# A transformer block's attention on one core: scores and transposed probabilities move into shared PSUM banks

## The chip, the cores and the metric

The kernel runs on one core of a Trainium2 chip. The metric is the device time of one execution in microseconds; three timed runs of the kernel before gave 797.0, 797.51 and 798.45, median 797.51. A core has five engines with an instruction queue each: TensorE (PE, matmuls; PEld is its loading of weights), VectorE (DVE), ScalarE (ACT), GpSimd (POOL) and SyncE (SP, which here only issues DMA transfers). They run side by side and wait for each other by semaphores. Matmuls write to PSUM, which has eight banks of 512 fp32 numbers for each of the 128 partitions.

## The reference, cut to what matters

One layer on 512 tokens of 2048 numbers: a norm, sliding-window attention with a gate, a projection back, then a second stage that adds a gated embedding, and a last norm. The attention has 32 query heads in 4 groups of 8, each group with one head of keys and values, 64 numbers a head:

```python
q, k, v, gate = jnp.split(h @ w_in, [...], axis=-1)
scores = jnp.einsum('bnqhgd,bnjhd->bnhgqj', q, kb) * (SWA_HEAD_DIM ** -0.5) + bias
scores = jnp.where(mask, scores, jnp.finfo(jnp.float32).min)      # a window of 128 keys
m = jnp.maximum(scores.max(axis=-1, keepdims=True), sink)
e = jnp.exp(scores - m)
probs = e / (e.sum(axis=-1, keepdims=True) + jnp.exp(sink - m))
out = jnp.einsum('bnhgqj,bnjhd->bnqhgd', probs, vb).reshape(bsz, seq, SWA_WIDTH)
y = (out * jax.nn.silu(gate)) @ w_out
```

## The kernel before

**Precision.** Every fp32 operand is split into a high and a low part, and a product is three matmuls (`mm3`, L126 to L128). The split of a weight piece is one ScalarE cast (`whi`, L109) and one VectorE subtraction (`wlo`, L110).

**Stages.** A first stage projects keys, values and two query blocks (until about 70 us). Then come 30 more projection blocks of queries (`qps`) and gates (`gps`), each 16 times `mm3`: 40 of these `mm3` by themselves, and the other 432 but 8 as filling between the steps of attention, so that TensorE has work while the softmax runs on other engines. Behind attention (from about 450 us) stand the output projection, the embedding's stage and the last norm.

**Attention** has 64 blocks of work (4 key heads x 16 units of 32 query tokens x 8 heads). The loop at L909 makes 67 steps; step `i` issues, in this order:

- the value matmuls of an output block (`weigh`, L586, even steps): two passes, with the high and the low part of the transposed probabilities `r`;
- the transposes of block `i-2` (`turn`, L546), two matmuls on TensorE that write `pt`; ScalarE copies it as the high part of `r` (L557), VectorE subtracts for the low part (L558);
- the scores of block `i` (`scores`, L478), two matmuls into `s`, one bank each;
- VectorE's softmax on `s`: add the bias (L508), subtract and find the minimum (L511, one for each half), merge (L516); later ScalarE's exponentials (L522), VectorE's reciprocal (L524), ScalarE's scaling to `pr` (L533 to L537, in the step after);
- 6 `mm3` of the projections (7 from step 30 on), and between them, at places counted by `n`, a weight split, the second part of the output (`own`, L589), its evaluation (L598 on ScalarE, L600 on VectorE), and the **pieces**: what a finished projection block still needs on VectorE and ScalarE. A query block has three pieces: scale (`qps`, L325, VectorE), high part (`q`, L336, ScalarE), low part (L334, VectorE). A gate has three too (L630, L631, L624), and later a fourth. Pieces wait in two lists, `chores` and `idle`, and `some()` issues the first of a list. Before, a step issues one at n = 0, one at n = 2 if more than one waits, and one at n = 4.

The order of the work on all five engines is written out by this loop, and each engine runs its own instructions strictly in that order. The pool library puts in the semaphores.

**Banks.** Pool `psum` has two banks each for the tags `o`, `p` and `t` (outputs, projections, transposes); one more pool of two banks holds the scores: one set of two banks, used by every step.

**Sums of weights.** Some weights are added on the way (`sum_weights`, L688): SP copies 512 KB from HBM to HBM (L693), and GpSimd's queue adds a second block to it (L695). Eight of these copies are issued before attention (SUMS_EARLY = 16), the others in its steps. SP's queue holds the loads of weights (`wraw`, L102) as well.

Of the kernel before, what the change touches and what calls it, by code (L numbers as in the profile page):

```python
# [55 lines left out]
def trunk_kernel(ctx: ExitStack, tc: tile.TileContext, a: dict):  # L56
# [8 lines left out]
    psum = pool("psum", bufs=2, space=PSUM)  # L65

    banks_s = ExitStack()
    others = {"s": banks_s.enter_context(tc.tile_pool(name="psum_s", bufs=2, space=PSUM))}

    pn = const.tile([P, KC], F32, name="pn")  # L70

# [338 lines left out]

    pre.close()
    banks_s.close()
    spsum = mid.enter_context(tc.tile_pool(name="psum_w", bufs=1, space=PSUM))
    apool = mid.enter_context(tc.tile_pool(name="attn", bufs=1, reuse_waits="tile"))


# [1 line left out]

    U, T, PT, gates, biases = {}, {}, {}, {}, {}

    DV = apool.tile([P, NB - 1, 2, KVH * 2 * HD], F32R, name="DV")
    apool.tile([P, 8], F32, name="pad2")
# [36 lines left out]
    def scores(i):  # L461

        d, g = divmod(i, UNITS)
        if g == UNITS // 2 and d + 1 < KVH:
            load_bias(d + 1)
        of_keys = K[d].rearrange("p j l k -> p (j l k)")  # L470

        s_ps = spsum.tile([P, 2, S], F32, tag="w", name=f"s{i}")
        number = [min(2 * g + u + 1, GROUP + 1) * QB for u in range(2)]
        for u in range(2):
            first, n = max(2 * g + u - GROUP, 0), number[u]
            part, at = divmod(2 * g + u, S // QB // len(Q[d]))
            st = Q[d][part][:, at].rearrange("p h q -> p (h q)")
            nc.tensor.matmul(s_ps[:, u, : 2 * n], st, of_keys[:, first * 2 * QB : (first * QB + n) * 2], start=True, stop=True)  # L478
        W = KEYS + 2
        t = apool.tile([P, 2, W], F32, tag="t", name=f"t{i}", bufs=2)  # L480
        at = t[:, 0, 0:1]

        def two(of, stride, n):
            return bass.AP(tensor=at.tensor, offset=at.offset + of, ap=[at.ap[0], [stride, 2], [1, n]])

        def by_block(out, u, n):
            of = s_ps[:, u, : 2 * n].rearrange("p (j l k) -> p l j k", l=2, k=QB)
            return out.rearrange("p (j k) -> p j k", k=QB), of[:, 0], of[:, 1]

        late = QB if g >= P // TQ else 0  # L490
        seen = [t[:, 0, 0 : P + 1], t[:, 1, 1 + late : P + 2 + late] if late else t[:, 1, 0 : P + 1]]
        pr = [t[:, u, 1 + late * u : 1 + late * u + P] for u in range(2)]
        nc.gpsimd.tensor_copy(two(0, W + W - 1 if late else W, 1), sinkb[:, d : d + 1].unsqueeze(1).to_broadcast([P, 2, 1]))  # L493
        for u, n in enumerate(number):
            if n < P:
                nc.gpsimd.memset(t[:, u, 1 + n : 1 + P], -MASKED)
        yield
        bias = biases[d][:, ::-1]
        sm = apool.tile([P, 24], F32, tag="sm", name=f"sm{i}", bufs=4)
        if not late:  # L500
            for u, n in enumerate(number):
                blocks_of, high, low = by_block(t[:, u, 1 : 1 + n], u, n)
                nc.vector.tensor_add(blocks_of, high, bias[:, KEYS - n :].rearrange("p (j k) -> p j k", k=QB))
        else:
            x = t[:, :, 1 : 1 + KEYS].rearrange("p u (j k) -> p u j k", k=QB)
            of = s_ps[:, :, : 2 * KEYS].rearrange("p u (j l k) -> p u l j k", l=2, k=QB)
            spread = bias.rearrange("p (j k) -> p j k", k=QB).unsqueeze(1).to_broadcast([P, 2, KEYS // QB, QB])
            nc.vector.tensor_add(x, of[:, :, 0], spread)  # L508
        for u, n in enumerate(number):
            blocks_of, high, low = by_block(t[:, u, 1 : 1 + n], u, n)  # L510
            nc.vector.tensor_tensor_reduce(  # L511
                out=blocks_of, in0=low, in1=blocks_of, scale=-1.0, scalar=sinkb[:, d : d + 1], op0=ALU.add, op1=ALU.min,
                accum_out=sm[:, u : u + 1],
            )
        if late:
            nc.vector.tensor_tensor(  # L516
                out=two(1, W + P, QB), in0=t[:, :, 1 : 1 + QB], in1=t[:, :, 1 + P : 1 + KEYS], op=ALU.min
            )
        yield
        for u in range(2):  # L520
            su = seen[u]
            nc.scalar.activation(su, su, AF.Exp, scale=-1.0, bias=sm[:, u : u + 1], accum_out=sm[:, 2 + u : 3 + u])  # L522
        yield
        nc.vector.reciprocal(sm[:, 4:6], sm[:, 2:4])  # L524
        yield

        T[i] = apool.tile([P, 2, P], F32, tag="pr", name=f"pr{i}", bufs=2)
        for u in range(2):
            out, src, w = T[i][:, u], pr[u], sm[:, 4 + u : 5 + u]
            ahead = 2 * (g + u) % GROUP * QB if late else 0  # L530
            if ahead == P // 2:
                out = out.rearrange("p (h k) -> p h k", h=2)[:, ::-1]
                nc.scalar.mul(out, src.rearrange("p (h k) -> p h k", h=2), w)  # L533
            else:
                nc.scalar.mul(out[:, ahead:], src[:, : P - ahead], w)  # L535
                if ahead:
                    nc.scalar.mul(out[:, :ahead], src[:, P - ahead :], w)  # L537

    def turn(i):


        d, g = divmod(i, UNITS)
        pr = T.pop(i)
        pt = bank(f"pt{i}", "t")[:, :256]
        for u in range(2):
            nc.tensor.transpose(pt[:, u * P : (u + 1) * P], pr[:, u, :], ident)  # L546

        j, part = divmod(i, 2)
        if part == 0:
            own = None  # L550
            if g >= P // TQ:
                own = apool.tile([P, 2, S], F32R, tag="own", name=f"own{j}")
            PT[j] = apool.tile([P, 2, S], F32R, tag="r", name=f"r{j}"), own
        r, own = PT[j]
        rh, rl = (r[:, l].rearrange("p (h t u q) -> p t u h q", h=GROUP, t=2, u=2)[:, part] for l in range(2))
        src = pt.rearrange("p (u h q) -> p u h q", u=2, h=GROUP)
        nc.scalar.copy(rh, src)  # L557
        nc.vector.tensor_sub(rl, src, rh.bitcast(F32))  # L558
        yield
        b = j % 2  # L560
        flat = lambda v, rows: v[rows].rearrange("p l (h t q) -> p t (l h) q", h=GROUP, t=2)[:, part]
        if own is not None:
            rows = slice(0, P) if b else slice(0, HB)
            sign = -1 if b else 1
            nc.gpsimd.affine_select(  # L565
                out=flat(own, rows), in_=flat(r, rows).bitcast(F32), pattern=[[0, 2 * GROUP], [sign, TQ]],
                compare_op=ALU.is_ge, fill=0.0, base=(-HB - 1 if b else 0) + sign * part * TQ, channel_multiplier=-sign,
            )
        yield
        if own is not None:  # L570
            here, there = slice(HB, P), slice(0, HB)
            if not b:
                here, there = there, here
            nc.scalar.copy(flat(own, there)[:, :GROUP], flat(own, here)[:, GROUP:].bitcast(F32))
# [110 lines left out]
                copies.append((t, block(nm, *first, jj, m) if first else summed[nm, {6: 7, 4: 6}[p], jj, m]))  # L685
                adds.append((t, block(nm, *{7: (2, 2), 5: (1, 2), 6: (1, 1), 4: (2, 1)}[p], jj, m)))
    SUM_STEPS = 2 * len(copies) + 6
    SUMS_EARLY = 16  # L688

    def sum_weights(i):  # L690

# [194 lines left out]
    for n in range(AHEAD):  # L886
        next(proj)
        if n % 4 == 3 and W.todo:
            W.todo.pop(0)()
        if n >= 2 * KC or n >= KC and n % 2:  # L890
            some(chores)
        if n >= 6 and n % 4 == 2 and n // 4 <= SUMS_EARLY // 2:
            sum_weights(2 * (n // 4 - 1))
    blocks = KVH * UNITS

    def sums_in(i):


        if i == 0:
            return ()  # L900
        if i < 4:
            return range(4 * i + 3, min(4 * i + 7, SUMS_EARLY), 2)
        n, of = SUM_STEPS - SUMS_EARLY, blocks - 4
        return range(SUMS_EARLY + (i - 4) * n // of, SUMS_EARLY + (i - 3) * n // of)

# [2 lines left out]
    softmax = iter(())  # L908
    for i in range(blocks + 3):  # L909

        before, softmax = softmax, scores(i) if i < blocks else iter(())
        turned = turn(i - 2) if 2 <= i < blocks + 2 else iter(())
        value = weigh(i // 2 - 2) if 4 <= i and i % 2 == 0 else iter(())
# [11 lines left out]
        for n in range(max(todo, 6)):  # L925
            if n < todo:
                next(proj)
            if n == 0:
                first_chores(i, 1)
                some(W.todo)  # L930
                some(chores or idle)
            elif n == 1:
                next(value, None)
            elif n == 2:
                if len(chores) > 1:
                    some(chores)
            elif n == 3:
                next(turned, None)
                next(value, None)
                next(softmax, None)  # L940
            elif n == 4:
                first_chores(i, 2)
                some(chores or idle)
            elif n == 5:
                next(softmax, None)
# [6 lines left out]
        some(chores or idle)  # L952
    during.close()
    mid.close()
    others["s"] = pool("psum_s2", space=PSUM, bufs=2, reuse_waits="tile")

    late = pool("late", reuse_waits="tile")
    rooms.append(late)
# [512 lines left out]
```

## Time and profile before

| | |
|---|---|
| median of three runs | 797.51 us |
| the profiled execution: its time | 797.58 us |
| its span | 795.9 us |
| TensorE, busy | 783.1 us (98%) |
| VectorE, busy | 590.7 us (74%) |
| ScalarE, busy | 517.4 us (65%) |
| granted TensorE clock, mean | 0.997 |

The span goes from the first to the last instruction; 1.7 us of the time lie around it. A row of the timeline gives the start in us, the duration in us, the engine, the line, the operation, what is written from what, the shape, and a count where equal instructions were put together; in square brackets stands how long the engine had been idle and what ended that. The starts of matmuls tell the pace: two of 512 columns start 0.23 us apart, though each is listed with 0.39.

### The profile page before, as it was taken

What the parts mean: (1) busy time and instruction counts of PE and PEld (TensorE: products, weight loads), DVE (VectorE), ACT (ScalarE), POOL (GpSimd) and SP (SyncE); (2) the same over time, 40 slices, a digit from 0 to 9 for tenths busy, and PEclk for the clock granted to TensorE, in tenths of its full rate; (3) what the DMA queues carried; (4) which work ended last, traced back from release to release, by engine and by line L of the source; (5) the groups of instructions that cost most, each with busy time, mean ns of one, the idle gap of its engine ahead of it and who ended that gap; (6) DMA issues with size and microseconds to landing.
All of it is one profiled execution on the core that took longest, in us unless ns stands there. A gap on an engine that the chain in (4) does not pass through costs nothing.

```text
span 795.9 us, 11177 instructions
## 1 busy us (share of the span) xinstructions
PE 783.1 (98%) x3658; PEld 649.4 (82%) x3658; DVE 590.7 (74%) x1171; ACT 517.4 (65%) x1131; POOL 141.7 (18%) x252
## 2 busy tenths in 40 slices
PE   9999999999999999999999999999999999999995
PEld 8888887878787888888888888888888888888885
DVE  4538567877887678776768799778867756988896
ACT  6635367876777667775767645456689656656765
POOL 0031122332243313341323100000000020210000
PEclk9999999999999999999999999999999999999998
DMA  9787779999899979889878498667873996796633
GB/s 349 231 227 262 204 181 283 296 237 285 242 254 260 249 227 249 240 235 274 241 201 181 126 367 317 224 208 233 286 243 127 348 201 201 162 230 208 190 106 106
DMA packets 44618, 184.87 MB, mean 232 GB/s; under 512 B 6720, under 2 KB 7232, under 8 KB 39440
## 3 DMA queue, kind: packets, MB, share of 16 engines
q1 hardware_dynamic: 36480, 142.94, 52.2%
q0 software_dynamic: 8080, 41.22, 27.4%
q8 instruction: 29, 0.48, 0.2%
q14 instruction: 29, 0.24, 0.1%
HBM read 177.26 MB, written 62.97 MB: 302 GB/s over the span
## 4 chain that ended last, share of the span: by engine, by line
PE 92%; DVE 4%; ACT 2%; DMA 1%; issue 1%; SPq 0%; ACTq 0%; DVEq 0%
PE gps L126 7%; PE gps L127 7%; PE gps L128 7%; PE qps L126 6%; PE qps L127 6%; PE qps L128 6%; PE g L128 5%; PE o L128 5%; PE g L127 5%; PE o L127 5%; PE o L126 5%; PE g L126 5%; PE vps L286 2%; PE s L478 2%; PE o L586 2%; PE pt L546 1%
## 5 line engine op out<-in xcount | busy, mean ns | idle before, releaser
L731 ACT CAST bhi<-braw 128x1024 fp32r<-128x1024 f32 x102 | 107.3, 1052 | 76.7 <-PE o L128 22.3
L732 DVE TENSOR_TENSOR blo<-braw,bhi 128x1024 fp32r<-128x1024 f32 x102 | 124.4, 1222 | 41.9 <-ACT bhi L731 41.5
L126 PE MATMUL gps<-xh,whi 128*128 128x512 f32 x256 | 100.5, 393 | 0.0
L127 PE MATMUL gps<-xl,whi 128*128 128x512 f32 x256 | 100.0, 391 | 0.0
L128 PE MATMUL gps<-xh,wlo 128*128 128x512 f32 x256 | 99.8, 390 | 0.0
L126 PE MATMUL qps<-xh,whi 128*128 128x512 f32 x224 | 87.6, 391 | 0.0
L127 PE MATMUL qps<-xl,whi 128*128 128x512 f32 x224 | 87.5, 391 | 0.0
L128 PE MATMUL qps<-xh,wlo 128*128 128x512 f32 x224 | 87.2, 389 | 0.0
L110 DVE TENSOR_TENSOR wlo<-wraw,whi 128x1024 fp32r<-128x1024 f32 x60 | 74.9, 1249 | 15.2 <-ACT whi L109 14.0
L126 PE MATMUL g<-bhi,fhg 128*128 128x512 f32 x192 | 75.1, 391 | 0.0
L126 PE MATMUL o<-bhi,fho 128*128 128x512 f32 x192 | 74.8, 390 | 0.0
L128 PE MATMUL g<-bhi,flg 128*128 128x512 f32 x192 | 74.8, 389 | 0.0
L128 PE MATMUL o<-bhi,flo 128*128 128x512 f32 x192 | 74.8, 389 | 0.0
L127 PE MATMUL g<-blo,fhg 128*128 128x512 f32 x192 | 74.7, 389 | 0.0
L127 PE MATMUL o<-blo,fho 128*128 128x512 f32 x192 | 74.7, 389 | 0.0
L109 ACT CAST whi<-wraw 128x1024 fp32r<-128x1024 f32 x60 | 62.3, 1040 | 11.7 <-issue 6.9
L565 POOL TENSOR_SCALAR_AFFINE_SELECT own<-r 64x512 fp32r<-64x512 f32 (+1 forms) x48 | 34.4, 716 | 163.1 <-DVE r L558 98.4
L493 POOL COPY t<-sinkb 128x2 f32<-128x2 f32 x64 | 41.3, 646 | 108.6 <-ACT pr L535 39.4
L558 DVE TENSOR_TENSOR r<-pt,r 128x256 fp32r<-128x256 f32 x64 | 27.1, 424 | 45.0 <-ACT r L557 44.2
L128 PEld LDWEIGHTS gps<-xh,wlo 128*128 128x128 f32 x256 | 48.1, 188 | 10.3
L126 PEld LDWEIGHTS gps<-xh,whi 128*128 128x128 f32 x256 | 48.1, 188 | 8.9
L127 PEld LDWEIGHTS gps<-xl,whi 128*128 128x128 f32 x256 | 48.1, 188 | 8.7
(230 smaller groups left out, 1730.2 us busy)
## 6 DMA issues: line engine op xcount, KB each, us to landing
w_out<-in_w_out POOLq DMA_DIRECT2D x32, 512.0 KB, 8.3
wraw<-in_w_gate_in SPq DMA_DIRECT2D x32, 512.0 KB, 7.1
braw<-w_out SPq DMA_DIRECT2D x32, 512.0 KB, 4.5
wraw<-in_w_q SPq DMA_DIRECT2D x28, 512.0 KB, 7.4
braw<-in_ple_gate SPq DMA_DIRECT2D x24, 512.0 KB, 4.3
braw<-in_w_out SPq DMA_DIRECT2D x22, 512.0 KB, 4.0
xw<-in_first SPq DMA_DIRECT2D x14, 640.5 KB, 6.4
w_out<-in_w_out SPq DMA_DIRECT2D x16, 512.0 KB, 8.8
```

Of the source, the lines that this page charges most:

```text
L109: nc.scalar.copy(hi, raw)
L110: nc.vector.tensor_sub(lo, raw, hi.bitcast(F32))
L126: nc.tensor.matmul(ps, sh, mh, start=first, stop=False, skip_group_check=more)
L127: nc.tensor.matmul(ps, sh, ml, start=False, stop=False, skip_group_check=more)
L128: nc.tensor.matmul(ps, sl, mh, start=False, stop=last, skip_group_check=more)
L286: nc.tensor.matmul(v_ps[t], h[:, c], part_of(high_at, 256, 512), start=f, stop=e, skip_group_check=True)
L478: nc.tensor.matmul(s_ps[:, u, : 2 * n], st, of_keys[:, first * 2 * QB : (first * QB + n) * 2], start=True, stop=True)
L493: nc.gpsimd.tensor_copy(two(0, W + W - 1 if late else W, 1), sinkb[:, d : d + 1].unsqueeze(1).to_broadcast([P, 2, 1]))
L558: nc.vector.tensor_sub(rl, src, rh.bitcast(F32))
L565: nc.gpsimd.affine_select(out=flat(own, rows), in_=flat(r, rows).bitcast(F32), pattern=[[0, 2 * GROUP], [sign, TQ]], compare_op=ALU.is_ge, ...
L731: nc.scalar.copy(hi, raw)
L732: nc.vector.tensor_sub(lo, raw, hi.bitcast(F32))
```

## The change

Scores and transposed probabilities of a step now live in one tile of two banks. Half `u` of the tile holds the 288 columns of scores of block `i`, and behind them, in columns 288 to 415, the 128 columns of transposed probabilities of block `i-2`, half `u`. Two such tiles are used in turn; the tag `t` of the pool `psum` goes, so that the eight banks are again all in use. The pieces are handed out differently: an even step (which evaluates an output) issues one, at n = 4; an odd step issues up to three, at n = 0, 2 and 4. The evaluation of an output moves from n = 3 to n = 2. Ten copies instead of eight are issued before attention, the first of them at n = 2 instead of 6. (Line numbers here are those before the change; behind the loop's head they move by two to four.)

```diff
-    others = {"s": banks_s.enter_context(tc.tile_pool(name="psum_s", bufs=2, space=PSUM))}
+    others = {v: banks_s.enter_context(tc.tile_pool(name=f"psum_{v}", bufs=2, space=PSUM)) for v in "ts"}
...
-    spsum = mid.enter_context(tc.tile_pool(name="psum_w", bufs=1, space=PSUM))
+    spsum = mid.enter_context(tc.tile_pool(name="psum_w", bufs=2, space=PSUM))
...
     def scores(i):
-        s_ps = spsum.tile([P, 2, S], F32, tag="w", name=f"s{i}")
+        s_ps = steps[i]
...
     def turn(i):
-        pt = bank(f"pt{i}", "t")[:, :256]
+        pt = steps[i + 2][:, :, 2 * KEYS : 2 * KEYS + P]
         for u in range(2):
-            nc.tensor.transpose(pt[:, u * P : (u + 1) * P], pr[:, u, :], ident)
+            nc.tensor.transpose(pt[:, u], pr[:, u, :], ident)
...
-        src = pt.rearrange("p (u h q) -> p u h q", u=2, h=GROUP)
+        src = pt.rearrange("p u (h q) -> p u h q", h=GROUP)
         nc.scalar.copy(rh, src)
         nc.vector.tensor_sub(rl, src, rh.bitcast(F32))
...
-    SUMS_EARLY = 16
+    SUMS_EARLY = 20
...
-        if n >= 6 and n % 4 == 2 and n // 4 <= SUMS_EARLY // 2:
-            sum_weights(2 * (n // 4 - 1))
+        if n % 4 == 2 and n // 4 < SUMS_EARLY // 2:
+            sum_weights(2 * (n // 4))
...
     for i in range(blocks + 3):
+        if i < blocks + 2:
+            steps[i] = spsum.tile([P, 2, S], F32, tag="w", name=f"w{i}")
...
             if n == 0:
                 first_chores(i, 1)
                 some(W.todo)
-                some(chores or idle)
+                if i % 2 or i >= blocks:
+                    some(chores or idle)
             elif n == 1:
                 next(value, None)
             elif n == 2:
-                if len(chores) > 1:
-                    some(chores)
+                next(value, None)
+                if i % 2:
+                    some(chores or idle)
             elif n == 3:
                 next(turned, None)
-                next(value, None)
                 next(softmax, None)
...
-    others["s"] = pool("psum_s2", space=PSUM, bufs=2, reuse_waits="tile")
+    for v in "ts":
+        others[v] = pool(f"psum_{v}2", space=PSUM, bufs=2, reuse_waits="tile")
```

**TensorE at the start of step 40.** `o18` is an output block, `r18` the transposed probabilities it uses, `pr38` the probabilities of block 38, `k2` and `q2` keys and queries; in brackets stand the engines whose semaphores the instruction waits for. Before:

```order
L586 MATMUL o18_3330<-r18_3216,V0_730 128x512 [waits Activation_49]
L586 MATMUL o18_3330<-r18_3216,V0_730 128x512 [waits DVE_49]
L546 MATMUL pt38_3333<-ident_82,pr38_3286 128x128 [waits Activation_49] x2
L478 MATMUL s40_3349<-k2_2164,q2_1_2137 128x288 [waits DVE_49,PE_49]
L478 MATMUL s40_3349<-k2_2164,q2_1_2137 128x288
L126 MATMUL qps13_3320<-xh2_216,whi36_3239 128x512
```

Now:

```order
L586 MATMUL o18_3298<-r18_3184,V0_733 128x512 [waits Activation_49]
L586 MATMUL o18_3298<-r18_3184,V0_733 128x512
L546 MATMUL w40_3297<-ident_85,pr38_3252 128x128 [waits PE_49,Activation_49]
L546 MATMUL w40_3297<-ident_85,pr38_3252 128x128 [waits Activation_49]
L478 MATMUL w40_3297<-k2_2152,q2_1_2126 128x288 [waits DVE_49]
L478 MATMUL w40_3297<-k2_2152,q2_1_2126 128x288
L126 MATMUL qps13_3288<-xh2_219,whi36_3206 128x512
```

The order of the matmuls is the same. Transposes and scores write one tile, `w40`. The score's wait for VectorE is for another count: before it was the last read of `s39` in step 39 (L511); now it is the subtraction of this step (L558), which reads the transposes of `w40`. The second value matmul no longer waits.

**VectorE from step 12 to step 13.** `u0` is the evaluated output, `qps7` a query block, `r5` the transposed probabilities. Before:

```order
L110 TENSOR_TENSOR wlo16_1721<-wraw16_1662,whi16_1720 128x1024
L325 SCALAR_TENSOR_TENSOR qps7_1556<-qps7_1556,rb_132 128x512
L600 TENSOR_TENSOR u0_1224<-o4_1689,tmp0_4_1738 64x4x64
L600 TENSOR_TENSOR u0_1224<-o4_1689,tmp1_4_1739 64x4x64
L334 TENSOR_TENSOR q1_1086<-qps7_1556,q1_1086 64x32x16 x2
L524 RECIPROCAL sm12_1709<-sm12_1709 128x2
L558 TENSOR_TENSOR r5_1696<-pt11_1757,r5_1696 128x2x8x16
```

Now:

```order
L110 TENSOR_TENSOR wlo16_1718<-wraw16_1660,whi16_1717 128x1024
L600 TENSOR_TENSOR u0_1231<-o4_1688,tmp0_4_1728 64x4x64
L600 TENSOR_TENSOR u0_1231<-o4_1688,tmp1_4_1729 64x4x64
L325 SCALAR_TENSOR_TENSOR qps7_1556<-qps7_1556,rb_135 128x512
L524 RECIPROCAL sm12_1706<-sm12_1706 128x2
L558 TENSOR_TENSOR r5_1694<-w13_1749,r5_1694 128x2x8x16
```

The low part of the query block (L334) has left the even step; it now stands in step 13, behind the softmax's reads of the scores. ScalarE's high part (L336) has moved with it.

**SP's queue ahead of attention.** `wraw` are weight pieces, `small` and `w_out` the copies. Before:

```order
L693 DMA small_7_1_783<-in_w_out 16x8192
L102 DMA wraw4_887<-in_w_q 128x1024
L693 DMA w_out_7_0_0_784<-in_w_out 16x8192
L693 DMA w_out_7_0_1_785<-in_w_out 16x8192
L102 DMA wraw5_921<-in_w_q 128x1024
```

Now:

```order
L693 DMA small_7_1_787<-in_w_out 16x8192
L693 DMA w_out_7_0_0_788<-in_w_out 16x8192
L102 DMA wraw4_892<-in_w_q 128x1024
L693 DMA w_out_7_0_1_789<-in_w_out 16x8192
L693 DMA w_out_7_0_2_790<-in_w_out 16x8192
L102 DMA wraw5_926<-in_w_q 128x1024
```

Each of these weight loads now has one more copy ahead of it.

More of the change, by code (lines that the diff above doesn't have):

```diff
@@ L412, in trunk_kernel @@
     banks_s.close()
-    spsum = mid.enter_context(tc.tile_pool(name="psum_w", bufs=1, space=PSUM))
+    spsum = mid.enter_context(tc.tile_pool(name="psum_w", bufs=2, space=PSUM))
     apool = mid.enter_context(tc.tile_pool(name="attn", bufs=1, reuse_waits="tile"))
-    U, T, PT, gates, biases = {}, {}, {}, {}, {}
+    U, T, PT, gates, biases, steps = {}, {}, {}, {}, {}, {}
     DV = apool.tile([P, NB - 1, 2, KVH * 2 * HD], F32R, name="DV")
@@ L901, in sums_in @@
         if i < 4:
-            return range(4 * i + 3, min(4 * i + 7, SUMS_EARLY), 2)
+            return range(4 * i + 3, 4 * i + 7 if i < 3 else SUMS_EARLY, 2)
         n, of = SUM_STEPS - SUMS_EARLY, blocks - 4
```

## The prediction

> **What bounds the kernel now.** I read the page first, then who waited for whom on TensorE, then single steps of attention in order of time.
>
> The page's first part (busy us, share of the span, instructions):
>
> ```profile
> PE 783.1 (98%) x3658; PEld 649.4 (82%) x3658; DVE 590.7 (74%) x1171; ACT 517.4 (65%) x1131; POOL 141.7 (18%) x252
> ```
>
> TensorE is at work for 783.1 of 795.9 us. A change that leaves its matmuls as they are, as this one does, can gain only what TensorE waits, and every new wait of TensorE is paid in full. Its waits inside attention, and the one row that tells how promptly ScalarE picks up the transposed probabilities (us in total, times, longest):
>
> ```profile
> PE o L586 <- DVE r L558: 1.8, 3, 1.0
> PE s L478 <- DVE sm L511: 1.5, 4, 0.4
> ACT r L557 <- PE pt L546: 45.4, 36, 2.3
> ```
>
> In 36 of 64 steps ScalarE stands ready and waits for the transposes; in the other 28 it comes late. Now two undisturbed steps, 40 (even) and 41 (odd), in order of time (start us, us, engine, line):
>
> ```profile
> 304.34 0.63 PE L586 MATMUL o<-r,V 128*128 128x512 f32 x2
> 304.81 0.38 PE L546 MATMUL pt<-ident,pr 128*128 128x128 f32 x2
> 304.92 0.30 PEld L478 LDWEIGHTS s<-k,q 128*128 128x128 f32 x2
> 304.95 0.51 PE L478 MATMUL s<-k,q 128*128 128x288 f32 x2
> 305.23 0.37 ACT L557 CAST r<-pt 128x256 fp32r<-128x256 f32 x1 [0.77 <-PE pt L546]
> 305.70 0.43 DVE L558 TENSOR_TENSOR r<-pt,r 128x256 fp32r<-128x256 f32 x1 [0.65 <-ACT r L557]
> 306.05 0.45 DVE L508 TENSOR_TENSOR t<-s,bias 128x288 f32<-128x288 f32 x1
> ...
> 310.34 0.38 PE L546 MATMUL pt<-ident,pr 128*128 128x128 f32 x2
> 310.45 0.30 PEld L478 LDWEIGHTS s<-k,q 128*128 128x128 f32 x2
> 310.76 0.37 ACT L557 CAST r<-pt 128x256 fp32r<-128x256 f32 x1 [0.79 <-PE pt L546]
> ...
> 311.17 0.43 DVE L558 TENSOR_TENSOR r<-pt,r 128x256 fp32r<-128x256 f32 x1 [0.44 <-ACT r L557]
> ```
>
> The reader is to see that TensorE goes from the transposes to the scores without a pause (weights of the scores at 304.92, 0.11 us behind the first transpose), while ScalarE's copy and VectorE's subtraction read the transposes from `pt`, a bank of their own, until 306.13.
>
> **What the change takes away.** The rows of the four spots where TensorE now stands still (steps 6, 14, 22 and 30):
>
> ```profile
> 125.53 0.40 PE L586 MATMUL o<-r,V 128*128 128x512 f32 x1
> 126.46 0.42 DVE L558 TENSOR_TENSOR r<-pt,r 128x256 fp32r<-128x256 f32 x1
> 126.94 0.50 PE L586 MATMUL o<-r,V 128*128 128x512 f32 x1 [1.01 <-DVE r L558]
> 127.28 0.44 PE L546 MATMUL pt<-ident,pr 128*128 128x128 f32 x2
> 128.09 0.50 PE L478 MATMUL s<-k,q 128*128 128x288 f32 x2 [0.37 <-DVE sm L511]
> 128.44 0.39 PE L126 MATMUL qps<-xh,whi 128*128 128x512 f32 x1
> 128.67 0.40 PE L127 MATMUL qps<-xl,whi 128*128 128x512 f32 x1
> ...
> 166.79 0.40 PE L586 MATMUL o<-r,V 128*128 128x512 f32 x1
> ...
> 168.61 0.50 PE L478 MATMUL s<-k,q 128*128 128x288 f32 x2 [0.37 <-DVE sm L511]
> ...
> 207.17 0.81 PE L586 MATMUL o<-r,V 128*128 128x512 f32 x2
> ...
> 208.63 0.50 PE L478 MATMUL s<-k,q 128*128 128x288 f32 x2 [0.37 <-DVE sm L511]
> ...
> 247.33 0.40 PE L586 MATMUL o<-r,V 128*128 128x512 f32 x1
> 248.24 0.50 PE L586 MATMUL o<-r,V 128*128 128x512 f32 x1 [0.51 <-DVE r L558]
> 248.58 0.45 PE L546 MATMUL pt<-ident,pr 128*128 128x128 f32 x2
> 249.40 0.50 PE L478 MATMUL s<-k,q 128*128 128x288 f32 x2 [0.37 <-DVE sm L511]
> ```
>
> In step 40 the first value pass stands 0.61 us ahead of the scores (304.34 to 304.95). Here it is 2.56 us (125.53 to 128.09), 1.82, 1.46 and 2.07: 1.95, 1.21, 0.85 and 1.46 us lost, together 5.5 us. Each spot comes two steps behind an even step (4, 12, 20, 28) in which VectorE and ScalarE had the evaluation of an output block, a weight split and all three pieces of a query block, and the lag reached TensorE only then. The change hands out one piece in an even step and three in an odd one, which has no output to evaluate: the 5.5 us go. The new order gives the scores two sets of banks, too, so that the second of the two waits named above has no reason left. I take the whole 5.5 as gain; it can't be more, since no other wait of this kind stands in attention.
>
> **What it adds.** In a step the program first issues the transposes, the copy (L557) and the subtraction (L558), then the scores. With both in one tile, the scores are written into the same two banks that these two engines are to read. The built program orders the score matmul behind VectorE, at the count that this same step's subtraction sets; and the second value pass loses its own wait for that subtraction, because a wait ahead of it on TensorE now covers it. So between the transposes and the scores TensorE has to stand until the subtraction has ended. Behind the waiting matmul on TensorE's queue stand the projection's matmuls, which could have run: nothing hides it.
>
> Price of one: the subtraction ends at 306.13 in step 40; a TensorE matmul that waited for it started 0.06 us behind its end (126.88 to 126.94); so the scores' weights would load at 306.19 and not 304.92: 1.27 us. In step 41, 311.60 plus 0.06 less 310.45: 1.21. The first and the last of the 62 steps (2 to 63) that have both transposes and scores:
>
> ```profile
> 106.87 0.30 PEld L478 LDWEIGHTS s<-k,q 128*128 128x128 f32 x2
> 107.59 0.42 DVE L558 TENSOR_TENSOR r<-pt,r 128x256 fp32r<-128x256 f32 x1 [2.27 <-ACT r L557]
> ...
> 433.53 0.30 PEld L478 LDWEIGHTS s<-k,q 128*128 128x128 f32 x2
> 434.24 0.42 DVE L558 TENSOR_TENSOR r<-pt,r 128x256 fp32r<-128x256 f32 x1 [0.42 <-ACT r L557]
> ```
>
> They give 1.20 and 1.19. I take 1.22 a step: 62 x 1.22 = 75.6 us. Below 62 x 1.19 = 73.8 it can't fall much, since each part (0.31 us until ScalarE starts, 0.37, 0.43 and the handing over) is read with the engines idle. It grows wherever ScalarE or VectorE come late. Over the same 62 steps the subtraction ends 109.4 us in all behind the scores' start; with 0.09 each for the hand-over and the weights ahead, 115 us is the upper end, if every lateness of today stayed.
>
> I don't think that it stays. The wait ties TensorE to the subtraction once a step, so no lag is carried over, and each step gets 1.2 us longer for the same work of the other engines. The stretches of attention (us, then busy us of PE, PEld, DVE, ACT, POOL; the clock; DMA share and GB/s):
>
> ```profile
> 106.00:248.00 142.00, 139.34 (x657) 113.74 (x655) 109.51 (x311) 103.90 (x309) 42.99 (x76) 1.00 0.97 264
> 248.00:445.00 197.00, 196.39 (x926) 162.56 (x927) 143.81 (x396) 137.30 (x396) 61.36 (x106) 1.00 0.87 231
> ```
>
> The first holds about 28 such steps: with 28 x 1.22 = 34 us more and 5 fewer it would be 171 long, and VectorE 64% busy instead of 77%, ScalarE 61%. VectorE loses something, since its first read of the scores (306.05) will have to wait for their end, some 0.6 us behind the wait; that is half of what the step gains. For late remains in steps that still hold a key or query block beside an output I add 1 us.
>
> [...]
>
> **The rest.** Ten copies of the sums' weights in place of eight are issued before attention, each ahead of a weight load on SP's queue. There the DMA engines are full:
>
> ```profile
> 90.00:95.00 5.00, 5.00 (x24) 4.14 (x23) 0.80 (x2) 1.38 (x5) 0.00 (x0) 1.00 1.02 270
> ```
>
> A copy reads and writes 512 KB each, so two more are 2.1 MB, 7.8 us at 270 GB/s. A weight load is asked for two pieces of 24 matmuls ahead, 24 x 0.23 = 5.5 us each (128.44 to 128.67 is one matmul), so 11 us cover it: nothing on the path, 7.8 at most if the cover were gone. The sooner output evaluation (one projection block earlier) lies on ScalarE and VectorE alone: nothing.
>
> Sum, against the profiled execution's own 797.58 us (797.51 is the median of the runs, so the same): 797.58 - 5.5 + 75.6 + 1 = **868.7 us**, 8.9% slower.
>
> **Rivals.**
>
> *Lag stays (907 us, 13%).* Steps in which ScalarE is late stay late, at the price of all 62 gaps of today: 797.58 + 115 - 5.5 = 907. For it: 28 of 64 copies are late now. Against it: the longer step, and the evener shares. Parts of it are likely, so the range leans up.
>
> *The wait is over before it counts (792 us, 5%).* If the count that the scores wait for belonged to an older reading of that set, two steps back, it would long be reached, TensorE would go on at 304.92 as now, and only the 5.5 us remain: 792.1. It decides by whether the subtraction of the same step has to end before the scores; banks without sharing show no such wait now, which is all that speaks for it. The order of the program speaks against it.
>
> *The clock falls (above 900 us, 4%).* TensorE would idle 1.2 of every 6.5 us, for the length of attention. If that took the granted clock to half for a tenth of the stretch from 98 to 434 us, 34 us come on top: 902. Against it: the clock is 1.00 in the stretch that holds all four spots, and after idling 1.0 and 0.4 us (126.94, 128.09) matmuls followed 0.23 apart. [...]
>
> **How the numbers follow.** Likeliest, 78%: the bare chain in each step, 862 to 878. With the rivals at 13, 5 and 4%, the range goes from 860 to 886: below, 62 x 1.13 (434.66 less 433.53, with no hand-over at all) less 5.5 gives 862, and 2 us are left for what I can't name; above, it takes in 17 us of the 39 between 75.6 and 115. About 0.2% (1.6 us) is what can be told from no change. Faster has only the third mechanism, 5%; within 0.2% nothing but mishap, 1%; slower 94%.
>
> **What would show it.** Right: TensorE waits at the scores for VectorE's subtraction (L558's new line), 62 times, shown as 0.9 to 1.0 us each (the transposes are listed as busy for 0.27 us of the 1.2) and some 60 in total; every step 1.2 us longer than now, evenly; no waits at the value passes; the stretch after attention as long as now; clock 1.00. Wrong: scores that start 0.03 us after the second transpose (rival two); waits of 2 us and over in many steps with ScalarE's copy starting long after the transposes (rival one); matmuls 0.4 us apart (rival three); waits for weight splits before 98 us (copies).

## The result, and the profile after

The changed kernel takes 869.41 us (median; 868.5 to 870.99) against 797.42 before: a ratio of 1.0896, 95% interval 1.0882 to 1.091. The forecast was 868.7.

Where the time went shows in three stretches: up to the first scores, attention, and all behind the last transposes. The view gives the stretch in us, its length, then the busy us of PE, PEld, DVE, ACT and POOL, the granted clock, the share of the DMA engines and GB/s. Before:

```profile
0.00:98.00 98.00, 97.15 (x472) 81.81 (x473) 52.91 (x99) 47.94 (x87) 14.54 (x40) 1.00 0.80 257
98.00:444.40 346.40, 343.13 (x1617) 282.40 (x1616) 256.94 (x722) 246.81 (x717) 107.60 (x189) 1.00 0.90 241
444.40:795.90 351.50, 342.81 (x1573) 285.22 (x1571) 280.88 (x350) 222.69 (x328) 19.52 (x23) 0.99 0.70 217
```

After:

```profile
0.00:98.00 98.00, 97.15 (x470) 81.79 (x471) 52.87 (x99) 48.05 (x87) 14.54 (x40) 1.00 0.83 267
98.00:516.00 418.00, 358.19 (x1617) 284.77 (x1616) 253.61 (x723) 246.14 (x717) 103.09 (x189) 1.00 0.75 197
516.00:867.50 351.50, 342.80 (x1573) 285.32 (x1571) 281.15 (x350) 222.82 (x328) 19.53 (x23) 0.99 0.70 217
```

Attention is 71.6 us longer, with the same 1617 matmuls in it; the stages on either side are as long as they were. TensorE's busy time there grew by 15 us without more work: one transpose is listed with 0.27 us in both kernels, but before the scores started 0.03 us behind the second one and covered most of that time, and now nothing does until the wait is over (0.24 us for each of 62 steps). The clock is 1.00 as before. The waits after (us in total, times, longest):

```profile
ACT r L557 <- PE w L546: 105.0, 55, 3.1
...
PEld w L478 <- DVE r L558: 74.4, 62, 2.2
...
PE w L478 <- DVE r L558: 59.8, 62, 1.9
```

The two waits of before, at the value passes and the scores, are gone; in their place stands one, 62 times, the scores for the subtraction of the same step. The matmuls show 59.8 us of it and their weight loads 74.4; the transposes are still listed as busy for the difference. ScalarE now stands ready for the transposes in 55 of 64 steps, where it was 36. Step 40 in order of time:

```profile
346.46 0.63 PE L586 MATMUL o<-r,V 128*128 128x512 f32 x2
...
346.94 0.38 PE L546 MATMUL w<-ident,pr 128*128 128x128 f32 x2
347.35 0.37 ACT L557 CAST r<-w 128x256 fp32r<-128x256 f32 x1 [3.08 <-PE w L546]
...
347.83 0.42 DVE L558 TENSOR_TENSOR r<-w,r 128x256 fp32r<-128x256 f32 x1 [1.12 <-ACT r L557]
...
348.31 0.30 PEld L478 LDWEIGHTS w<-k,q 128*128 128x128 f32 x2 [1.23 <-DVE r L558]
348.31 0.53 PE L478 MATMUL w<-k,q 128*128 128x288 f32 x2 [0.99 <-DVE r L558]
...
348.94 0.46 DVE L508 TENSOR_TENSOR t<-w,bias 128x288 f32<-128x288 f32 x1 [0.69 <-PE w L478]
```

The scores' weights load 1.37 us behind the first transpose (346.94 to 348.31); before it was 0.11. So this step lost 1.26 us, and VectorE idles 0.69 us until the scores are there.

### The profile page after: what moved, and what is told of

Its sections match the earlier page's. It is cut to its first block, busy times and chain, and to the rows that moved or that the text cites. A ratio compares the mean times of both kernels' runs of the same rounds, so it can differ in the third digit from the quotient of the medians.

```text
span 867.5 us, 11177 instructions
## 1 busy us (share of the span) xinstructions
PE 798.1 (92%) x3658; PEld 651.9 (75%) x3658; DVE 587.6 (68%) x1171; ACT 517.0 (60%) x1131; POOL 137.2 (16%) x252
## 4 chain that ended last, share of the span: by engine, by line
PE 90%; DVE 4%; ACT 3%; DMA 2%; issue 1%; SPq 0%; DVEq 0%; ACTq 0%
PE gps L126 7%; PE gps L127 7%; PE gps L128 7%; PE qps L127 6%; PE qps L126 6%; PE qps L128 6%; PE g L127 5%; PE g L126 5%; PE o L126 5%; PE o L127 5%; PE o L128 5%; PE g L128 5%; PE w L478 4%; DVE r L558 3%; ACT r L557 3%; PE vps L286 2%
## 5 line engine op out<-in xcount | busy, mean ns | idle before, releaser
L558 DVE TENSOR_TENSOR r<-w,r 128x256 fp32r<-128x256 f32 x64 | 27.2, 424 | 92.2 <-ACT r L557 92.1
L478 PE MATMUL w<-k,q 128*128 128x288 f32 (+8 forms) x128 | 32.6, 336 | 59.8 <-DVE r L558 59.8
L557 ACT CAST r<-w 128x256 fp32r<-128x256 f32 x64 | 23.8, 372 | 105.8 <-PE w L546 105.0
L565 POOL TENSOR_SCALAR_AFFINE_SELECT own<-r 64x512 fp32r<-64x512 f32 (+1 forms) x48 | 47.4, 987 | 230.0 <-PE o L589 125.0
L478 PEld LDWEIGHTS w<-k,q 128*128 128x128 f32 x128 | 19.2, 188 | 74.6 <-DVE r L558 74.4
L522 ACT ACTIVATE t<-t,sm 128x129 f32<-128x129 f32 x128 | 50.5, 397 | 11.0 <-DVE t L516 9.1
```

The costliest lines, as they stand in the source:

```text
L565: nc.gpsimd.affine_select(out=flat(own, rows), in_=flat(r, rows).bitcast(F32), pattern=[[0, 2 * GROUP], [sign, TQ]], compare_op=ALU.is_ge, ...
```

## The experiments

The theory was that the whole loss is one wait: the scores are issued behind two readers of their own banks. The rivals were that sharing banks costs by itself, that the new hand-out of the pieces or the early sums carry part of it, and that late engines or the clock make the wait longer.

**The sharing undone.** The kernel before, with the hunks of the diff on pieces, evaluation and sums, but with `pt` and `s` in banks of their own.

```diff
-        pt = steps[i + 2][:, :, 2 * KEYS : 2 * KEYS + P]
+        pt = bank(f"pt{i}", "t")[:, :256]
...
-        s_ps = steps[i]
+        s_ps = spsum.tile([P, 2, S], F32, tag="w", name=f"s{i}")    # psum_w with bufs=1
```

> Undoes the sharing alone: the transposes have their own banks again and the scores one set of two, while the new hand-out of the pieces, the earlier evaluation and the ten early copies stay. Theory (the wait of the scores for the subtraction is the whole loss, and the hand-out takes the four waits of before away): 792.0, that is 797.5 less 5.5, and no waits at the value passes or the scores over 0.3 us. Rival one (the new hand-out or the early copies cost time themselves): over 798. Rival two (the second set of score banks is what takes the four waits away): about 795, with the scores' waits of 0.67 us at the four spots still there.

It took 796.27 us, ratio 0.9976 (0.9966 to 0.9985). So the sharing carries the loss: 73 us between two kernels that differ in it alone. But only 1.5 of the 5.5 us came. In its trace TensorE waits 1.1 us at step 6 and then runs 3.4 us at a clock of 0.51 (rows in the last section). Ahead of that stands a load of weights for which ScalarE stands still for 4.5 us in step 4:

```profile
ACT whi L109 <- DMA wraw<-in_w_gate_in: 4.5, 1, 4.5
```

Before, no wait for a load of this weight is longer than 0.6. That made the early sums a suspect.

**The sharing alone.** The changed kernel with pieces, evaluation and sums as before.

```diff
             if n == 0:
...
-                if i % 2 or i >= blocks:
-                    some(chores or idle)
+                some(chores or idle)
...
-    SUMS_EARLY = 20
+    SUMS_EARLY = 16
```

> The sharing alone: scores and transposes in one tile, two tiles in turn, with the pieces, the evaluation and the copies as before the change. Theory: 62 waits of the scores at 1.22 us, the four old waits gone into these, and some late subtractions behind the even steps with three pieces, 797.5 - 5.5 + 75.6 + 6 = 874 (870 to 880), the lateness at steps 5, 13, 21 and 29. Rival (the hand-out of the pieces carries part of the loss): under 855.

It took 902.16 us, ratio 1.1306 (1.1285 to 1.1326). That is 28 us over what was expected of it and 33 over the changed kernel. The waits at the scores, then steps 12 and 13 of its trace:

```profile
PE w L478 <- DVE r L558: 81.6, 62, 4.3
```

```profile
176.51 0.46 DVE L508 TENSOR_TENSOR t<-w,bias 128x288 f32<-128x288 f32 x1 [0.69 <-PE w L478]
...
177.82 1.22 DVE L110 TENSOR_TENSOR wlo<-wraw,whi 128x1024 fp32r<-128x1024 f32 x1
...
178.95 0.69 DVE L325 SCALAR_TENSOR_TENSOR qps<-qps,rb 128x512 f32<-128x512 f32 x1
179.68 1.18 ACT L336 CAST q<-qps 64x512 fp32r<-64x512 f32 x2 [2.67 <-DVE qps L325]
180.61 0.38 PE L546 MATMUL w<-ident,pr 128*128 128x128 f32 x2
...
181.18 0.74 ACT L598 COPY tmp<-o 64x256 f32<-64x256 f32 x2
...
182.73 0.35 ACT L557 CAST r<-w 128x256 fp32r<-128x256 f32 x1
182.82 1.39 DVE L334 TENSOR_TENSOR q<-qps,q 64x512 fp32r<-64x512 f32 x2
...
184.44 0.42 DVE L558 TENSOR_TENSOR r<-w,r 128x256 fp32r<-128x256 f32 x1
...
184.91 0.53 PE L478 MATMUL w<-k,q 128*128 128x288 f32 x2 [3.92 <-DVE r L558]
```

In step 12 ScalarE idles 2.67 us at the first piece of a query block, because VectorE can scale it only behind the softmax and a weight split; behind it on ScalarE's queue stand the output's copies and the exponentials, and behind these the copy of step 13's transposes, 2.1 us behind them where 0.4 is usual (346.94 to 347.35 in step 40 above). VectorE then has the third piece ahead of the subtraction. Before the change such a lag was carried over to the next step and cost TensorE about 1.4 us a spot; here it falls on the very instruction that TensorE waits for, every time. Against the changed kernel that is 81.6 - 59.8 = 22 us. The rest, about 11, I put down to the clock, as an estimate from the rows that follow: behind the wait of step 13 TensorE ran at 0.51 for 3.4 us. Attention as a whole, then the stretches around step 13's wait:

```profile
98.00:541.10 443.10, 361.45 (x1581) 286.73 (x1580) 250.68 (x716) 242.34 (x707) 103.92 (x188) 0.97 0.71 186
...
181.97:185.38 3.41, 0.47 (x3) 0.47 (x4) 2.79 (x6) 1.99 (x8) 0.45 (x1) 1.00 0.99 276
185.38:188.80 3.42, 3.42 (x10) 2.65 (x9) 1.48 (x7) 1.28 (x5) 1.20 (x3) 0.51 0.78 120
188.80:192.20 3.40, 3.01 (x14) 2.24 (x13) 0.00 (x0) 0.35 (x2) 0.00 (x0) 0.99 0.43 87
```

At a clock of 0.51 only 10 matmuls fall into 3.4 us, of which 8 start in it, where some 15 of 512 columns would at 0.23 us each. A mean of 0.97 over 443 us lacks some 13 us of full clock, and in a part of these TensorE stood waiting anyway. Against the changed kernel with the old sums (867.89, below), which differs in the hand-out alone, the new hand-out is worth 34 us with shared banks, six times what it is worth without, and by the same estimate about a third of that is the clock.

**Both writers first.** The changed kernel; `turn` yields behind the transposes, so that the scores are issued ahead of the copy and the subtraction. TensorE's order is the same.

```diff
             nc.tensor.transpose(pt[:, u], pr[:, u, :], ident)
+        yield
...
         next(turned, None)
         next(softmax, None)
         next(turned, None)
+        next(turned, None)
         next(before, None)
```

> The changed kernel with one thing moved: the scores' matmuls are issued ahead of ScalarE's copy and VectorE's subtraction of the same step instead of behind them. TensorE's order, the shared banks and every other order are the same; what changes is that the two readers now wait for the scores, and the scores for nobody in this step. Theory (the loss is this one wait): the 62 waits go, the copy starts some 0.3 us later than now, and the time is 792 to 794, faster than both kernels. Rival (sharing banks costs by itself, since TensorE writes where others read, or the clock or the longer tile's shapes matter): 830 or more.

It took 795.84 us, ratio 0.9972 (0.9961 to 0.9983): 2 us over the expected range, and 73.6 us less than the changed kernel for the order of four instructions. The shared banks, the two sets and the shapes have stayed, so they cost nothing that can be seen. The 62 waits are gone; one remains, 2.4 us, that again follows a late load (3.1 us, step 8).

**The subtraction twice.** The changed kernel, `nc.vector.tensor_sub(rl, ...)` repeated in each step; the same numbers are written again.

> The changed kernel with the subtraction done twice in each of the 64 steps (the same numbers are written again). Theory (TensorE stands until VectorE has read the shared banks for the last time): each of 62 waits grows by 0.43 to 0.47 us, 869.4 + 62 x 0.45 = 897 (894 to 901). Rival (the price is that of changing over between writers and readers of a bank, whatever they do): 869 to 873, since VectorE has 30% of its time free.

It took 896.63 us, ratio 1.124 (1.1218 to 1.1263), 27.2 more than the changed kernel: 0.44 for each of 62 steps. An even step of its trace:

```profile
363.41 0.38 PE L546 MATMUL w<-ident,pr 128*128 128x128 f32 x2
363.83 0.37 ACT L557 CAST r<-w 128x256 fp32r<-128x256 f32 x1 [3.09 <-PE w L546]
364.30 0.88 DVE L559 TENSOR_TENSOR r<-w,r 128x256 fp32r<-128x256 f32 x2 [1.13 <-ACT r L557]
365.24 0.30 PEld L478 LDWEIGHTS w<-k,q 128*128 128x128 f32 x2 [1.69 <-DVE r L559]
```

The pair ends at 365.18 and the scores follow 0.06 us behind. The price is VectorE's reading time, paid one to one.

**The early sums alone.** The kernel before, with `SUMS_EARLY = 20` and its two ranges.

> The kernel before with the earlier sums of weights alone (ten copies ahead of attention, the adds 15, 17 and 19 all behind step 3). With the own-bank kernel at 796.3 and not 792, and ScalarE there waiting 4.5 us for a weight load in step 4, the theory is now that the earlier sums crowd the DMA engines and cost about what the hand-out gains: 799 to 801, with a weight split that waits for its load at step 4. Rival (the early copies are free, the rest of the 5.5 us was never to be had): 797.5.

It took 803.77 us, ratio 1.0064 (1.0047 to 1.0081): 6 us slower, over what was expected. GpSimd's adds around step 3, before and here:

```profile
104.17 1.56 POOL L695 DMA_DIRECT2D w_out<-in_w_out  x2
108.72 0.77 POOL L695 DMA_DIRECT2D w_out<-in_w_out  x1 [0.23 <-issue]
```

```profile
104.02 1.58 POOL L695 DMA_DIRECT2D w_out<-in_w_out  x2
108.58 2.40 POOL L695 DMA_DIRECT2D w_out<-in_w_out  x3 [0.23 <-issue]
...
114.91 0.53 SPq L102 DMA_DIRECT2D wraw<-in_w_gate_in  x1
...
121.10 1.05 ACT L109 CAST whi<-wraw 128x1024 fp32r<-128x1024 f32 x1 [3.23 <-DMA wraw<-in_w_gate_in]
```

The changed range issues three adds behind step 3 in place of one. The load issued at 114.91 comes late, ScalarE waits 3.23 us for it, and everything behind it on ScalarE and VectorE is late for step 6, which was late already: its value passes now wait 1.66 and 1.74 us, where one waited 1.01. Behind them the clock is 0.50 for one stretch, where before it was 1.00 (130.40 to 133.80 in both):

```profile
130.40:133.80 3.40, 3.22 (x9) 2.67 (x10) 2.46 (x13) 3.02 (x10) 1.38 (x3) 0.50 0.86 360
```

At 0.50 these 3.4 us lack 1.7 us of full clock, so by that estimate up to 1.7 of the 6 us are the clock's. Whether the adds or the two more copies weigh more was not tried apart.

**Writers first, sums as before.** The kernel of the third experiment with `SUMS_EARLY = 16` and its old ranges.

> The kernel with the scores issued ahead of the readers, with the sums of weights as before the change (eight copies, one add behind step 3). Theory (sharing is free when both writers go first, and the early sums delay the weights at steps 4 to 8): 792 to 793, no wait of TensorE over 0.5 us in attention. Rival (something else of the sharing or of the hand-out costs 3 us): 795 to 797.

It took 792.22 us (791.82 to 792.46), ratio 0.9922 (0.9908 to 0.9935): faster than both kernels. TensorE waits nowhere in attention. Step 40:

```profile
299.00 0.38 PE L546 MATMUL w<-ident,pr 128*128 128x128 f32 x2
299.11 0.30 PEld L478 LDWEIGHTS w<-k,q 128*128 128x128 f32 x2
299.13 0.51 PE L478 MATMUL w<-k,q 128*128 128x288 f32 x2
299.74 0.37 ACT L558 CAST r<-w 128x256 fp32r<-128x256 f32 x1 [2.04 <-PE w L478]
300.21 0.42 DVE L559 TENSOR_TENSOR r<-w,r 128x256 fp32r<-128x256 f32 x1 [0.38 <-ACT r L558]
300.56 0.45 DVE L508 TENSOR_TENSOR t<-w,bias 128x288 f32<-128x288 f32 x1
```

Now ScalarE waits for the scores, 0.3 us longer than it waited for the transposes, and that lies beside TensorE's next matmuls.

**The hand-out alone.** The kernel before with the hunks on pieces and evaluation; own banks, one set, old sums.

> The kernel before with the hand-out of the pieces and the earlier evaluation alone: own banks, one set for the scores, sums as before. Theory (the hand-out alone takes the four waits away, 797.5 - 5.5): 792. Rival one (early sums have nothing to do with it): 796. Rival two (the second set of score banks is needed for it): about 795, with waits of 0.67 us at the scores.

It took 792.35 us, ratio 0.9928 (0.991 to 0.9946). So the hand-out by itself brings what the forecast gave it, and the second set of score banks isn't needed for it.

**Writers first, pieces as before.** The sharing alone, with the yield of the third experiment.

> Shared banks with the scores issued ahead of the readers, and the pieces, the evaluation and the sums as before the change: against the sharing alone (902.2) it differs by the order of four instructions a step. Theory (the whole loss of sharing is in that order; the second set takes away the scores' waits of 0.67 us at four spots): 794 to 797.5. Rival (late ScalarE and VectorE hurt with shared banks in any order): 810 or more.

It took 796.12 us, ratio 0.9975 (0.9965 to 0.9985): 106 us less than the sharing alone. In this kernel, with shared banks too, late engines cost next to nothing, since TensorE doesn't wait for them in each step. It lies 1.7 us below the kernel before; its trace has no wait at the scores any more, 1.8 us at the value passes.

**The changed kernel with the old sums.**

> The changed kernel with the sums of weights as before the change. With own banks the earlier sums cost 3.9 us (796.3 against 792.35), alone 6. Theory (with sharing each step has 1.2 us more in which loads can land, so that only the late subtraction at step 5, 1.06 us, is theirs): 868 to 868.6. Rival (they cost the same whatever the step's length): 863 to 866.

It took 867.89 us (867.44 to 868.23), ratio 1.0877 (1.0861 to 1.0892). The early sums cost 1.5 us of the change's 72; in longer steps most of their lateness is covered (ScalarE waits 1.7 us for the late load in the changed kernel, 4.5 with own banks).

| banks, order | pieces | sums | us |
|---|---|---|---|
| own (the kernel before) | old | old | 797.4 to 797.8 |
| own | new | old | 792.35 |
| own | old | early | 803.77 |
| own | new | early | 796.27 |
| shared, readers first | old | old | 902.16 |
| shared, readers first | new | old | 867.89 |
| shared, readers first (the change) | new | early | 869.41 |
| shared, writers first | old | old | 796.12 |
| shared, writers first | new | early | 795.84 |
| shared, writers first | new | old | 792.22 |

## Why the prediction was right, point by point

- **The wait of the scores for the subtraction, 62 x 1.22 = 75.6 us: right.** Moving the scores ahead of the readers takes 73.6 us away, and 75.7 where both kernels have the old sums (867.89 to 792.22); doubling the last reader adds its duration 62 times. In step 40 the forecast was 1.27 us; 1.26 was measured. The waits shown, "0.9 to 1.0 us each" and "some 60 in total", came as 0.92 to 0.99 in most steps and 59.8 us in total.
- **The 5.5 us that go: right in size.** The hand-out alone brings 5.5 (797.81 to 792.35). The second set's share, which the text named as well, isn't needed for that; with the old hand-out it takes away the waits at the scores alone.
- **Who waits: in this kernel the order of issue sets it.** With the scores first, ScalarE's copy starts 0.3 us later in step 40, and TensorE does not wait. Whether the waiting could be left out for both sides was not tried.
- **The copies, "nothing on the path": wrong.** The early sums cost 1.5 us here, 3.9 with own banks, 3.6 with writers first and 6 alone; with own banks and alone, up to 1.7 of it, an estimate, is one stretch at a clock of 0.51 and 0.50. The text counted two copies ahead of attention and the cover of weight loads there, and left out the adds that move with them: three behind step 3, where the DMA engines are as full (1.00 of their time from 110 to 116 us in the kernel with early sums alone). Which of the two weighs more stays open. A moved range of a plan has to be read out step by step, on GpSimd's queue as on SP's.
- **"For late remains I add 1 us": right in size by luck.** The one late step of note is step 5: 1.0 us (a wait of 1.92 where 0.92 is usual), behind a late load of weights; with the old sums it is gone (longest wait 1.1 us). So this 1 us stands for what the early sums cost, which the text put at nothing.
- **"I don't think that it stays": right, but for a reason that was half wrong.** The text credited the step's extra 1.2 us and the wait that ends each lag. The sharing alone has both and took 902. It was the hand-out that kept ScalarE and VectorE on time. The rival of lags, priced at 907, comes near the 902 of the kernel without it, but partly by luck: it has 39 us more of waiting than the bare chain, and that kernel shows 22 us more than the changed one, and about 11 that I put down to the clock, which the price doesn't hold.
- **The rival of the clock: not in this kernel, but real.** It was given 4% and held nothing here: the clock is 1.00 in attention, through 62 waits listed with 0.92 to 1.92 us, and with the subtraction twice (62 waits, 1.5 us at most) its mean over the run is 0.997, as before. In the sharing alone (62 waits, 4.3 us at most) it is 0.97 over attention, and 0.51 for 3.4 us behind the wait of 3.92 us. The half clock that the rival supposes stands in no row of before; 0.50 and 0.51 came in three of the experiments.
- **The rival of a wait long over: refuted.** The wait is for the subtraction of the same step in all 62: the scores' weights load 0.05 to 0.06 us behind its end each time.
- Nothing outside attention moved, as said.

## What to carry to other kernels

When two results share a PSUM bank, issue all of TensorE's writes into it before the first reader. In this kernel only the readers waited then (ScalarE 2.04 us in step 40), and TensorE, the bound, ran on; the same banks in the order write, read, write cost 1.2 us for each turn. By such a wait an engine that was off the critical path became part of it, with all its lateness: an uneven hand-out of small work, 5.5 us without the wait, cost 34 with it. And a hunk that goes along "for free" (the early sums) is worth a run by itself: without it the mended kernel gains 5.6 us on the one before, with it 2.

## What the runs showed of the hardware

The clock of TensorE fell behind some waits and not behind others. In the kernel with its own banks and early sums, TensorE was busy for 2.04 of 3.40 us in one stretch, and ran the next 3.4 us at a clock of 0.51 (10 matmuls lie in them, and 18 in the 3.4 us behind):

```profile
125.70:129.10 3.40, 2.04 (x8) 0.91 (x7) 3.10 (x11) 2.05 (x8) 0.19 (x1) 1.00 1.00 302
129.10:132.50 3.40, 3.40 (x10) 2.71 (x9) 2.78 (x7) 2.66 (x10) 0.44 (x1) 0.51 1.10 388
132.50:135.90 3.40, 3.40 (x18) 2.78 (x17) 3.18 (x9) 3.10 (x9) 2.17 (x3) 0.99 1.09 413
```

In the kernel with both writers first and early sums, a longer wait, 2.41 us, lay across two such stretches, and the clock stayed at 1.00:

```profile
134.90:138.30 3.40, 2.67 (x14) 1.89 (x12) 0.18 (x1) 0.79 (x1) 0.60 (x2) 1.00 1.01 309
138.30:141.70 3.40, 1.72 (x7) 1.43 (x8) 2.77 (x4) 3.33 (x10) 0.00 (x0) 1.00 0.74 157
141.70:145.10 3.40, 3.40 (x17) 2.51 (x16) 2.36 (x8) 3.31 (x8) 1.93 (x3) 1.00 0.54 141
```

So the length of a wait does not settle it, and neither does the share shown as busy: 1.72 of 3.40 us kept the clock, and 2.04 lost it (a matmul is listed for longer than the 0.23 us until the next one starts). The sharing alone was busy for 0.47 of 3.41 us ahead of its 0.51 (step 13 above). In the changed kernel 62 waits of 0.92 to 1.92 us, one a step, left the clock at 1.00. What decides it was not shown.
